# Moving a kernel's weight splitting and elementwise work from GpSimd to ScalarE and VectorE

## The chip, the cores and the metric

The kernel runs on one core of one Trainium2 chip. Its time is the device time of one execution in microseconds (us), and the median over runs is compared. Five engines work side by side on the core, each through its own instructions in order: TensorE (PE, with its weight loads shown apart as PEld), VectorE (DVE), ScalarE (ACT), GpSimd (POOL) and SyncE (SP), which here issues most DMAs.

## The reference

Two layers over 512 latent and 256 context tokens of 2048 channels. Each layer normalizes, modulates (shift, scale and gate come from a product of a condition vector with `mod_w`), mixes tokens, and adds the gated result to its input.

```python
for i in range(DEPTH):                                   # 2 layers
    shift, scale, gate = jnp.split(sc @ mod_w[i] + mod_b[i], 3, axis=-1)
    h_lat = rms_norm(x, norm_g[i]) * (1.0 + scale[:, None]) + shift[:, None]
    ...
    if i % N_MIXERS == 0:
        y_lat, y_ctx = rglru_mixer(h_lat, h_ctx, ...)    # h @ w_in, 4-tap convolution, gates, two scans, @ w_out
    else:
        y_lat, y_ctx = diff_attn_mixer(h_lat, h_ctx, ...)  # h @ w_in, q/k norm, rotary, 2 softmaxes, @ w_out
    x = x + gate[:, None] * y_lat
```

## The kernel before

Every product with a large weight is made of three matmuls: a float32 value is split into a high part in the matmul's format (a cast) and a low part (the value minus the high part), and high x high, high x low and low x high are summed in PSUM. `split` (line 43) issues the two instructions, the cast at L47 if it goes to ScalarE or L49 if to another engine, and the subtraction at L50. `weights` (line 52) fetches one weight unit of 128 x 1024 floats (512 KB) by a DMA from SP's queue into a tile `raw` (two buffers), and splits it into `wh` and `wl` (five buffers each; in the attention one unit in six has a further pair). A `raw` buffer is free for the next DMA when the subtraction has read it.

The stages in order:

- The prologue makes the RMS rows and the shift and scale of the first layer, and starts the first projections.
- The first mixer (`phase1`) works channel block by channel block, 16 of them. For a block it projects two half-blocks (`proj`: 16 channel tiles, six matmuls each, lines L327 to L331), copies the first into a padded row `up`, convolves it over time with four taps (`lru_conv`: the first tap and the bias at L426, three more on VectorE at L428, then the split into `xh` and `xl`), multiplies by the gate weights (`gps`, lines L451 to L453, three matmuls for each of eight pieces), and goes through sigmoid, tanh, exp, square and square root on ScalarE and products and scans on VectorE (lines L455 to L481). The output of a block is multiplied by its gated half (`lru_out`, lines L489 to L495). Beside that VectorE sums the modulation of the second layer (`mod_vec`, L102, one weighted sum of 512 columns after the other), spread over the blocks.
- `phase2` multiplies by `w_out` (lines L557 to L559) in four column chunks, while VectorE sums the gate of the layer for the same chunk (L102 again); a matmul with ones (L522, `gps<-ma,ones`) ends each gate. Then come the norm and the transposes of the second layer (`h_evac`).
- `phase3` goes through 16 heads. For a head the projections (lines L692 to L694, `pj`) of k and v and then of q and the gate take four weight units each; between them stands the attention of the head before: scores (L755), softmax (L757 to L765), transposes (L778), products with v (lines L790 to L792). `qk_norm` norms q and k and applies rotary positions; its four products with the sine table are at L715.
- The last head runs beside the first output columns, and `phase4` makes the others.

The order on each engine is fixed when the program is built: a scheduler places instructions by a model of the engines, so a change of engine for one kind of work moves others too. Where a line below names `hi_eng` and `lo_eng`, it is the engines of the cast and of the subtraction: in general VectorE and GpSimd, in the attention VectorE for every second subtraction too, and beside the last head ScalarE for the cast.

Of the kernel before, what the change touches and what calls it, by code (L numbers as in the profile page):

```python
# [29 lines left out]
# the last head's attention and the units of the first output columns beside it ("."), in order:  # L30
# q: channels, s: scores, t: transposes, v: times v, o: back to rows, f: norm, y: output
# [5 lines left out]
class Kern:  # L37
# [5 lines left out]
    def split(self, raw, hi, lo, hi_eng, lo_eng):  # L43
        """raw (float32) == hi + lo, both float32r"""
        nc = self.nc
        if hi_eng is nc.scalar:
            nc.scalar.copy(hi, raw)  # L47
        else:
            hi_eng.tensor_copy(hi, raw)  # L49
        return lo_eng.tensor_tensor(lo, raw, hi.bitcast(F32), op=ALU.subtract)  # L50

    def weights(self, src, shape, hi_eng=None, lo_eng=None):
        """one weight unit [128, 1024] from DRAM, split in two"""
        nc, wp = self.nc, self.wp
        raw = self.raw()
        self.wdma = nc.sync.dma_start(raw, src)
        self.wn += 1
        if self.wx is not None and self.wn % 6 == 0:
            h = self.wx.tile([128, 1024], F32R, tag="whx", name="wh")
            l = self.wx.tile([128, 1024], F32R, tag="wlx", name="wl")  # L60
        else:
            h = wp.tile([128, 1024], F32R, tag="wh", bufs=5, name="wh")
            l = wp.tile([128, 1024], F32R, tag="wl", bufs=5, name="wl")
        self.split(raw, h, l, hi_eng or nc.vector, lo_eng or nc.gpsimd)
        f = lambda t: t.rearrange("p (k c) -> p k c", k=shape[0])
        return f(h), f(l)
# [7 lines left out]
    def rsqrt(self, pool, v, n, pre, bufs=1):  # L74
        """v ** -0.5 of a small tile: a guess from the bits of v, then Newton's steps"""
# [12 lines left out]
    def mod_vec(self, ch, pool, nm, bufs=1):  # L88
        """512 columns of silu(c) @ mod_w: sums over the channel tiles, one per partition"""
# [18 lines left out]
    def mod_stream(self, pool, chunks):  # L108
        """shift and scale of layer 1: four channel tiles per chunk"""
# [33 lines left out]
    def mod_cols(self, layer, part, ch):  # L143
        """sums of the partials, channel-major: [128 channels, (latent, context)] x 2"""
        nc = self.nc
        ps = self.psum("mcol")
        for s in range(2):
            nc.tensor.matmul(ps[:, 2 * s:2 * s + 2], part[:, 128 * s:128 * s + 128], self.sel, start=True, stop=True)
        for s in range(2):
            self.mod_col(layer, 2 * ch + s, ps[:, 2 * s:2 * s + 2])  # L150

# [52 lines left out]
    def htile(self, kt, g):  # L204
        """high and low parts of 128 channels of 384 tokens"""
        return self.hp.tile([128, 2, 384], F32R, tag=f"h{kt}{g}", name=f"h{kt}{g}")

    def h_evac(self, layer, kt, g, ps, pool):
        """h = rms * A + B for one channel tile of a token group; ps: the transposed rms rows"""
# [6 lines left out]
        self.split(t, h[:, 0, :], h[:, 1, :], nc.vector, nc.gpsimd if g and kt % 2 == 0 else nc.vector)  # L216

    def norm_group(self, layer, g, kts, xt, pool):
        """transposes the rms rows of three token tiles, for the channel tiles kts, into h"""
# [22 lines left out]
    def rows(self, t, unit):  # L242
        """rms rows of one token tile, transposed"""
# [30 lines left out]
    def pairs(self, pool, unit):  # L274
        """shift and scale of layer 0 for two channel tiles at a time; behind them, h of these
        tiles and their part of the first three half-blocks"""
# [69 lines left out]
    def phase1(self, early):  # L346
# [3 lines left out]
        with tc.tile_pool(name="p1", bufs=1, reuse_waits="tile") as pool:  # L350
# [8 lines left out]
            def padded(b, uo):  # L359
                """[2 zeros, latent, 4 zeros, context, 1 zero]"""  # L360
# [35 lines left out]
    def lru_consts(self, pool):  # L396
        nc, cp = self.nc, self.c1
        # 8 softplus(-lambda), both signs
# [22 lines left out]
    def lru_conv(self, b, u, pool):  # L421
# [4 lines left out]
        nc.gpsimd.tensor_scalar(xc, u[:, 2:2 + UL], cw[:, b, 2:3], self.convb[:, b:b + 1], op0=ALU.mult, op1=ALU.add)  # L426
# [5 lines left out]
    def lru_block(self, b, x, pool):  # L432
# [3 lines left out]
        if b % 2 == 0:  # L436
            raw = self.wp.tile([128, 1024], F32, tag="raw", bufs=2, name="graw")
            nc.sync.dma_start(raw, a["gate_w"][b // 2])
            self.gates = tl("gh", 1, 1024, F32R), tl("gl", 1, 1024, F32R)
            self.split(raw, *self.gates, nc.vector, nc.gpsimd)  # L440
# [18 lines left out]
        for d in range(2):  # L459
# [4 lines left out]
            # 1 - a^2 = tanh(-log a) (1 + a^2)  # L464
# [19 lines left out]
    def lru_out(self, b, go, pool):  # L484
        """y = (sum of both directions) * silu(g)"""
# [15 lines left out]
    def y_tiles(self, kts, pool):  # L501
        """the mixer's output back as tiles of h, split"""
# [11 lines left out]
    def mod_gate(self, layer, n, pool, nm, gbufs=1):  # L514
        """512 columns of the gate, on all partitions: [128, nm, 512]"""
# [9 lines left out]
    def gate_rows(self):  # L525
        """the gate of layer 1, one row of 256 columns after the other, to DRAM"""
# [106 lines left out]
    def att_tables(self, pool):  # L633
        """gain times cosine and sine for q and k, spilled: [128, cos q, sin q, cos k, sin k]"""
# [26 lines left out]
        # lambda and the output norm's gain  # L661
# [21 lines left out]
    def qkv_mm(self, w, t, ps=None, kts=range(KT)):  # L683
        """one token tile times 256 columns"""
# [12 lines left out]
    def qk_norm(self, raw, nt, nm):  # L697
        """RMS over the 64 of each head half, gain, rotary positions; raw [128, nt, 128] in place"""
# [14 lines left out]
        for h in range(2):  # L713
            for c in range(2):
                nc.gpsimd.tensor_tensor(tv[:, :, c, :, h, :], xv[:, 0:4, c, :, 1 - h, :], sv[:, :, :, h, :], op=ALU.mult)  # L715
# [6 lines left out]
    def k_channels(self, kraw, k):  # L722
        """k [128, 2 halves, 768]: half c has its high parts on its own 64 partitions, its low parts on the other 64"""
# [10 lines left out]
    def q_channels(self, qraw, q):  # L734
        """q [128 = (part 64, the same 64), (high, low), 2 halves, 512]"""
# [32 lines left out]
    def attend_t(self, qt, st):  # L768
        """the attention of one query tile, transposed and split: [128, (high, low), 6 key tiles, 2 query tiles, 128]"""
# [13 lines left out]
    def attend_v(self, v, st):  # L783
        """the outputs of two query tiles, transposed"""
# [12 lines left out]
    def attend_o(self, pair, st):  # L797
        """back to rows"""
# [41 lines left out]
    def ytiles(self, hd):  # L840
        """the tiles of one head's output: tokens 0-383, tokens 384-511"""
# [7 lines left out]
    def yload(self, u):  # L849
        """the outputs of heads 2u and 2u + 1, split"""  # L850
# [15 lines left out]
    def early_out(self):  # L866
        """the first output columns, from all heads but the last, for two pairs of token tiles"""
# [3 lines left out]
        for pair in ((0, 1), (2, 3)):  # L871
            acc = {t: self.ppool.tile([128, 512], F32, tag="pj", bufs=2, name="acc") for t in pair}
            for u in range(8):
                if pair[0] == 0:
                    self.yload(u)
                w = self.weights(a["w_o"][0, u], (2, 512), nc.scalar, nc.vector if u % 2 else None)
# [25 lines left out]
    def head(self, hd, prev, rest, done):  # L902
        """projections of head hd, between them the attention of the head before"""
# [55 lines left out]
        w = [self.weights(a["w_kv"][hd, u], (4, 256), None, nc.vector if u % 2 and hd else None) for u in range(4)]  # L959
# [42 lines left out]
        w = [self.weights(a["w_qg"][hd, u], (4, 256), None, nc.vector if u % 2 else None) for u in range(4)]  # L1002
# [64 lines left out]
def layout(inp):  # L1067
# [6 lines left out]
    # shift and scale of layer 0: [16 chunks, 4 units, 128, 4 k-tiles, 256]  # L1074
    o["mod_w"] = c(f["mod_w"][0, :, :4096].reshape(4, 4, 128, 16, 256).transpose(3, 0, 2, 1, 4))
    # gate of layer 0; shift, scale and gate of layer 1: [16 chunks, 8 units, 128, 2 k-tiles, 512]
# [4 lines left out]
    # half-blocks u0 g0 u1 g1 ..: [32, 2, 128, 8, 128]  # L1081
# [12 lines left out]
    # [4 column chunks, 8 units, 128, 2 k-tiles, 512]  # L1094
    wo = lambda w: c(w.reshape(8, 2, 128, 4, 512).transpose(3, 0, 2, 1, 4).reshape(4, 8, 128, 1024))
    o["w_o"] = wo(f["att_w_out"][0])
    # [16 heads, 4 units, 128, 4 k-tiles, (k, v) or (q, g)]
# [26 lines left out]
```

## Time and profile before

| | |
|---|---|
| Time, median of 3 runs (lowest, highest) | 2505.36 us (2503.09, 2505.61) |
| Profiled execution: span from first to last instruction | 2499.5 us |
| TensorE busy with matmuls | 2350.4 us, 94% of the span |
| VectorE busy | 1875.8 us, 75% |
| ScalarE busy | 858.5 us, 34% |
| GpSimd busy | 694.9 us, 28% |
| Mean granted TensorE clock | 0.975 of full speed |

The profiled execution has its span alone on record, 2499.5 us; it lies 5.9 us under the median of the runs, since the span begins with the first instruction and ends with the last. Busy shares are over the whole span, and the stages have different limits, so each stage is to be read by itself.

### The profile page before, as it was taken

The numbers are of one execution on the slowest core, as the hardware profiler recorded it, in microseconds if no ns is written. First come the engines' busy times: TensorE is split into PE (matmuls) and PEld (weight loads), VectorE is DVE, ScalarE is ACT, GpSimd is POOL, SyncE is SP. The second block draws the span as 40 slices with busy tenths as digits, with TensorE's granted clock in tenths as the row PEclk, the third lists the DMA queues.
The fourth block names the chain that finished last, engine by engine and source line by source line (L and its number), as shares of the span: only waits on it lengthen the run. The fifth ranks groups of instructions, "written<-read, shape, count | busy, mean of one in ns | idle before, by whom it ended". The sixth has DMA issues, their size and how long they took to land.

```text
span 2499.5 us, 39647 instructions
## 1 busy us (share of the span) xinstructions
PE 2350.4 (94%) x15744; PEld 2197.3 (88%) x15744; DVE 1875.8 (75%) x3292; ACT 858.5 (34%) x1826; POOL 694.9 (28%) x390
## 2 busy tenths in 40 slices
PE   5989998989889899799999999999999999998899
PEld 4679998989889788679999999999999999997687
DVE  6457999999997866786787777778677766767622
ACT  4346535435337100033333333333333333235400
POOL 1243343433332233333121111212121211211352
PEclk8999999999999999999999999999999999999999
DMA  9912344434333655431232232322222211213552
GB/s 355 364 60 89 125 127 135 133 125 135 129 122 108 232 191 176 144 119 58 70 97 65 89 98 62 92 81 85 89 81 89 80 52 57 68 43 115 181 184 76
DMA packets 106473, 298.83 MB, mean 120 GB/s; under 512 B 12320, under 2 KB 33072, under 8 KB 106288
## 3 DMA queue, kind: packets, MB, share of 16 engines
q1 hardware_dynamic: 101536, 287.33, 35.2%
q10 hardware_dynamic: 4752, 8.98, 1.0%
q8 instruction: 123, 2.02, 0.3%
q14 instruction: 62, 0.51, 0.1%
HBM read 277.45 MB, written 18.82 MB: 119 GB/s over the span
## 4 chain that ended last, share of the span: by engine, by line
PE 42%; DVE 9%; DMA 3%; issue 2%; ACT 1%; POOL 1%; SPq 0%; DVEq 0%; ACTq 0%; POOLq 0%
PE pj L694 9%; PE pj L693 9%; PE pj L692 9%; PE sc L755 3%; PE acc L557 2%; DVE wh L49 2%; PE acc L558 2%; PE acc L559 2%; PE atr L778 1%; DMA raw<-w_kv 1%; DVE wl L50 1%; DMA raw<-w_o 1%; PE o L792 1%; PE o L791 1%; PE o L790 1%
## 5 line engine op out<-in xcount | busy, mean ns | idle before, releaser
L50 POOL TENSOR_TENSOR wl<-raw,wh 128x1024 fp32r<-128x1024 f32 x202 | 533.8, 2643 | 1334.8 <-DVE wh L49 975.1
L692 PE MATMUL pj<-wh,h 128*128 128x256 f32 x2560 | 730.2, 285 | 3.3 <-DVE v L50 2.7
L694 PE MATMUL pj<-wh,h 128*128 128x256 f32 x2560 | 729.2, 285 | 0.2
L693 PE MATMUL pj<-wl,h 128*128 128x256 f32 x2560 | 729.1, 285 | 0.0
L692 PEld LDWEIGHTS pj<-wh,h 128*128 128x128 f32 x2560 | 489.9, 191 | 6.2 <-DVE v L50 2.9
L693 PEld LDWEIGHTS pj<-wl,h 128*128 128x128 f32 x2560 | 490.2, 192 | 4.5 <-issue 2.6
L694 PEld LDWEIGHTS pj<-wh,h 128*128 128x128 f32 x2560 | 490.2, 191 | 3.1 <-issue 0.4
L49 DVE CAST wh<-raw 128x1024 fp32r<-128x1024 f32 x256 | 212.6, 832 | 173.4 <-PE acc L559 82.0
L102 DVE SCALAR_TENSOR_TENSOR ma<-mw,scT,ma 128x512 f32<-128x512 f32 x360 | 310.5, 906 | 18.9 <-DMA mw<-mod_v 18.9
L327 PE MATMUL proj<-h,wh 128*128 128x384 f32 x1024 | 265.5, 340 | 6.9 <-DVE h L49 6.9
L329 PE MATMUL proj<-h,wh 128*128 128x384 f32 x1024 | 271.6, 337 | 0.0
L331 PE MATMUL proj<-h,wl 128*128 128x384 f32 x1024 | 270.4, 336 | 0.0
L327 PEld LDWEIGHTS proj<-h,wh 128*128 128x128 f32 x1024 | 185.5, 190 | 15.2 <-DVE h L49 11.1
L329 PEld LDWEIGHTS proj<-h,wh 128*128 128x128 f32 x1024 | 187.2, 189 | 4.2 <-issue 2.0
L331 PEld LDWEIGHTS proj<-h,wl 128*128 128x128 f32 x1024 | 186.9, 189 | 0.8 <-issue 0.8
L761 ACT ACTIVATE p<-sc,mx 128x768 f32<-128x768 f32 x128 | 114.5, 904 | 113.1 <-DVE mx L757 108.1
L557 PE MATMUL acc<-wh,h 128*128 128x512 f32 x384 | 152.4, 398 | 0.0
L757 DVE TENSOR_REDUCE mx<-sc 128x2 f32<-128x1536 f32 x64 | 112.1, 1752 | 52.5 <-PE sc L755 52.3
L558 PE MATMUL acc<-wl,h 128*128 128x512 f32 x384 | 150.4, 392 | 0.1
L559 PE MATMUL acc<-wh,h 128*128 128x512 f32 x384 | 149.8, 391 | 0.0
L47 ACT CAST athl<-atr 128x512 fp32r<-128x512 f32 (+1 forms) x128 | 55.7, 483 | 196.7 <-PE atr L778 196.5
L755 PE MATMUL sc<-k,q 128*128 128x512 f32 (+1 forms) x512 | 108.2, 339 | 2.5 <-ACT p L761 2.5
(241 smaller groups left out, 3942.8 us busy)
## 6 DMA issues: line engine op xcount, KB each, us to landing
mw<-mod_v SPq DMA_DIRECT2D x96, 512.0 KB, 3.8
mw<-mod_w SPq DMA_DIRECT2D x64, 512.0 KB, 9.8
raw<-w_in SPq DMA_DIRECT2D x64, 512.0 KB, 3.6
raw<-w_kv SPq DMA_DIRECT2D x64, 512.0 KB, 3.7
raw<-w_qg SPq DMA_DIRECT2D x64, 512.0 KB, 3.9
raw<-w_out SPq DMA_DIRECT2D x40, 512.0 KB, 4.3
raw<-w_o SPq DMA_DIRECT2D x40, 512.0 KB, 3.5
raw<-mod_v SPq DMA_DIRECT2D x64, 256.0 KB, 3.6
```

What stands on the lines that cost most here:

```text
L49: hi_eng.tensor_copy(hi, raw)
L50: return lo_eng.tensor_tensor(lo, raw, hi.bitcast(F32), op=ALU.subtract)
L102: nc.vector.scalar_tensor_tensor(acc[m], w[:, k, :], sc, acc[m], op0=ALU.mult, op1=ALU.add)
L327: nc.tensor.matmul(ps[g][:, :384], wh, h[g][:, 0, :], start=first, stop=False)
L329: nc.tensor.matmul(ps[g][:, :384], wh, h[g][:, 1, :], start=False, stop=False)
L331: nc.tensor.matmul(ps[g][:, :384], wl, h[g][:, 0, :], start=False, stop=last)
L557: nc.tensor.matmul(acc[t], yh, wh, start=(kt == first), stop=False)
L558: nc.tensor.matmul(acc[t], yh, wl, start=False, stop=False)
L559: nc.tensor.matmul(acc[t], yl, wh, start=False, stop=(kt == last))
L692: nc.tensor.matmul(ps, h[:, 0, c], wh, start=(kt == 0), stop=False)
L693: nc.tensor.matmul(ps, h[:, 0, c], wl, start=False, stop=False)
L694: nc.tensor.matmul(ps, h[:, 1, c], wh, start=False, stop=(kt == KT - 1))
```

## The change

Every weight unit is cast on ScalarE and its low part subtracted on VectorE, whatever the stage. The gate weights of the first mixer (`graw`) go the same way. The first convolution tap, until now a GpSimd instruction, becomes a ScalarE activation with scale and bias. The four sine products of `qk_norm` go to VectorE, and so does the low part of h in `h_evac` where GpSimd had it. GpSimd keeps memory sets at the start and the one-time tables of `att_tables`.

```diff
-    def weights(self, src, shape, hi_eng=None, lo_eng=None):
+    def weights(self, src, shape):
...
-        self.split(raw, h, l, hi_eng or nc.vector, lo_eng or nc.gpsimd)
+        self.split(raw, h, l, nc.scalar, nc.vector)
...
-        self.split(t, h[:, 0, :], h[:, 1, :], nc.vector, nc.gpsimd if g and kt % 2 == 0 else nc.vector)
+        self.split(t, h[:, 0, :], h[:, 1, :], nc.vector, nc.vector)
...
-        nc.gpsimd.tensor_scalar(xc, u[:, 2:2 + UL], cw[:, b, 2:3], self.convb[:, b:b + 1], op0=ALU.mult, op1=ALU.add)
+        nc.scalar.activation(xc, u[:, 2:2 + UL], AF.Identity, scale=cw[:, b, 2:3], bias=self.convb[:, b:b + 1])
...
-            self.split(raw, *self.gates, nc.vector, nc.gpsimd)
+            self.split(raw, *self.gates, nc.scalar, nc.vector)
...
-                nc.gpsimd.tensor_tensor(tv[:, :, c, :, h, :], xv[:, 0:4, c, :, 1 - h, :], sv[:, :, :, h, :], op=ALU.mult)
+                nc.vector.tensor_tensor(tv[:, :, c, :, h, :], xv[:, 0:4, c, :, 1 - h, :], sv[:, :, :, h, :], op=ALU.mult)
...
-                w = self.weights(a["w_o"][0, u], (2, 512), nc.scalar, nc.vector if u % 2 else None)
+                w = self.weights(a["w_o"][0, u], (2, 512))
...
-        w = [self.weights(a["w_kv"][hd, u], (4, 256), None, nc.vector if u % 2 and hd else None) for u in range(4)]
+        w = [self.weights(a["w_kv"][hd, u], (4, 256)) for u in range(4)]
...
-        w = [self.weights(a["w_qg"][hd, u], (4, 256), None, nc.vector if u % 2 else None) for u in range(4)]
+        w = [self.weights(a["w_qg"][hd, u], (4, 256)) for u in range(4)]
```

VectorE's order in one block of the first mixer, from the second convolution tap (`xc<-up`) to the output product (`sg`), before; `a` and `r` are tiles of the scans:

```order
L428 SCALAR_TENSOR_TENSOR xc<-up_1668,conv_wT,xc 128x772
L479 SCALAR_TENSOR_TENSOR a_3560<-a_3560,r_3506 128x512
L428 SCALAR_TENSOR_TENSOR xc<-up_1668,conv_wT,xc 128x772
L49 CAST wh<-raw 128x1024
L481 TENSOR_TENSOR a_3549<-a_3549,a_3560 128x772
L49 CAST xh<-xc 128x772
L50 TENSOR_TENSOR xl<-xc,xh 128x772
L49 CAST wh<-raw 128x1024
L492 SCALAR_TENSOR_TENSOR sg<-sg,proj 128x384 x2
L494 TENSOR_TENSOR sg<-a_3549,sg 128x512
```

The same place on VectorE in the change:

```order
L428 SCALAR_TENSOR_TENSOR xc<-up_1668,conv_wT,xc 128x772
L50 TENSOR_TENSOR wl<-raw,wh 128x1024
L479 SCALAR_TENSOR_TENSOR a_3560<-a_3560,r_3506 128x512
L428 SCALAR_TENSOR_TENSOR xc<-up_1668,conv_wT,xc 128x772
L481 TENSOR_TENSOR a_3549<-a_3549,a_3560 128x772
L49 CAST xh<-xc 128x772
L50 TENSOR_TENSOR xl<-xc,xh 128x772
L50 TENSOR_TENSOR wl<-raw,wh 128x1024
L492 SCALAR_TENSOR_TENSOR sg<-sg,proj 128x384 x2
L494 TENSOR_TENSOR sg<-a_3549,sg 128x512
```

Each cast of `raw` has made room for a subtraction that reads `raw` and `wh`; the recurrence around it stands as it did.

ScalarE's order at the same block, from the square root (L468) to the next block's gates (L455), before:

```order
L468 ACT_TABLE_LOAD
L468 ACTIVATE r_3505<-r_3505 128x772
L466 ACTIVATE sq<-a_3560 128x772
L468 ACTIVATE r_3506<-r_3506 128x772
L361 COPY up_1668<-proj 128x384
L362 COPY up_1668<-proj 128x128
L363 COPY up_1668<-proj 128x256
L489 ACT_TABLE_LOAD
L489 ACTIVATE sg<-proj 128x384 x2
L455 ACT_TABLE_LOAD
```

And in the change:

```order
L468 ACT_TABLE_LOAD
L468 ACTIVATE r_3505<-r_3505 128x772
L466 ACTIVATE sq<-a_3560 128x772
L47 CAST wh<-raw 128x1024
L361 COPY up_1668<-proj 128x384
L362 COPY up_1668<-proj 128x128
L363 COPY up_1668<-proj 128x256
L468 ACTIVATE r_3506<-r_3506 128x772
L426 ACTIVATE xc<-up_1668,conv_bT,conv_wT 128x772
L47 CAST wh<-raw 128x1024 x2
L489 ACT_TABLE_LOAD
L489 ACTIVATE sg<-proj 128x384 x2
```

Three weight casts and the first tap have come in, and the second square root has moved behind the copies into `up`.

## Rows read from the trace of the kernel before

**Rows 1.** The page: busy us, share of the span, instructions of each engine.

```profile
PE 2350.4 (94%) x15744; PEld 2197.3 (88%) x15744; DVE 1875.8 (75%) x3292; ACT 858.5 (34%) x1826; POOL 694.9 (28%) x390
```

**Rows 2.** Busy time by stretch: start:end, length, engines, clock, DMA share, GB/s.

```profile
165.80:372.80 207.00, 193.94 (x1074) 192.05 (x1072) 182.39 (x195) 118.49 (x157) 82.86 (x39) 0.96 0.34 111
372.80:741.40 368.60, 329.37 (x1826) 324.35 (x1824) 357.28 (x427) 162.27 (x216) 132.08 (x45) 0.94 0.41 131
...
786.00:1045.80 259.80, 252.91 (x1112) 207.91 (x1110) 188.95 (x238) 44.02 (x88) 77.56 (x31) 0.99 0.57 185
1045.80:1190.00 144.20, 122.20 (x819) 110.78 (x818) 111.41 (x193) 42.37 (x93) 52.07 (x32) 0.93 0.32 99
1190.00:2205.00 1015.00, 1002.60 (x8167) 985.58 (x8166) 754.63 (x1593) 334.58 (x943) 201.26 (x164) 1.00 0.25 77
2205.00:2360.00 155.00, 139.51 (x905) 123.44 (x904) 110.18 (x227) 69.56 (x166) 38.37 (x25) 0.97 0.34 107
```

**Rows 3.** Waits of PE, whole run: total us, times, longest us.

```profile
PE gps L451 <- DVE xh L49: 32.1, 9, 7.8
PE gps L522 <- DVE ma L102: 20.0, 2, 13.2
PE gps L452 <- DVE xl L50: 17.0, 12, 2.5
```

**Rows 4.** Two short stretches of the first mixer, columns as in rows 2.

```profile
300.00:331.00 31.00, 31.00 (x181) 31.00 (x180) 30.82 (x35) 14.46 (x20) 13.01 (x4) 1.00 0.39 120
373.00:380.00 7.00, 0.83 (x3) 0.43 (x2) 6.96 (x7) 0.00 (x0) 3.10 (x1) 0.81 0.50 150
```

**Rows 5.** Timeline of DVE in one block: start, us, what.

```profile
398.30 2.88 DVE L102 SCALAR_TENSOR_TENSOR ma<-mw,scT,ma 128x512 f32<-128x512 f32 x1
...
401.98 1.40 DVE L102 SCALAR_TENSOR_TENSOR ma<-mw,scT,ma 128x512 f32<-128x512 f32 x2
...
417.91 0.99 DVE L428 SCALAR_TENSOR_TENSOR xc<-up,conv_wT,xc 128x772 f32<-128x772 f32 x1
```

**Rows 6.** Timeline of POOL over the same time.

```profile
397.07 3.56 POOL L50 TENSOR_TENSOR wl<-raw,wh 128x1024 fp32r<-128x1024 f32 x1 [14.06 <-PE proj L331]
```

**Rows 7.** DVE by line, 372.9 to 741.4 (eight blocks): count, busy us, mean ns, idle before.

```profile
L102 DVE SCALAR_TENSOR_TENSOR ma<-mw,scT,ma 128x512 f32<-128x512 f32 x184 | 153.8, 874 | 8.8 <-DMA mw<-mod_v 8.8
L428 DVE SCALAR_TENSOR_TENSOR xc<-up,conv_wT,xc 128x772 f32<-128x772 f32 x25 | 37.5, 1500 | 0.0
L49 DVE CAST wh<-raw 128x1024 fp32r<-128x1024 f32 x33 | 22.3, 677 | 0.0
L467 DVE SCALAR_TENSOR_TENSOR r<-sq,r 128x772 f32<-128x772 f32 x16 | 21.8, 1362 | 0.0
L494 DVE TENSOR_TENSOR sg<-a,sg 128x512 f32<-128x512 f32 x8 | 17.6, 2196 | 0.3
L475 DVE TENSOR_TENSOR_SCAN a<-a,r 128x512 f32<-128x512 f32 x8 | 16.2, 2025 | 0.0
L50 DVE TENSOR_TENSOR xl<-xc,xh 128x772 fp32r<-128x772 f32 x8 | 15.8, 1979 | 0.3
...
L479 DVE TENSOR_TENSOR_SCAN a<-a,r 128x512 f32<-128x512 f32 x9 | 11.4, 1271 | 0.0
...
L481 DVE TENSOR_TENSOR a<-a,a 128x772 f32<-128x772 f32 x8 | 7.6, 948 | 0.0
```

**Rows 8.** Groups by line, whole run: POOL's sine products for k, ACT's cast.

```profile
L715 POOL TENSOR_TENSOR rt<-kraw,tab 128x128 f32<-128x128 f32 x64 | 41.9, 684 | 173.6 <-ACT kraw L968 93.6 <-DVE l L762 79.9
...
L47 ACT CAST wh<-raw 128x1024 fp32r<-128x1024 f32 x16 | 16.8, 1050 | 16.9 <-DMA raw<-w_o 15.4 <-POOL rt L715 1.4
```

**Rows 9.** The chain that ended last: a subtraction on DVE with POOL idle.

```profile
1983.15 1.23 DVE wl L50
```

**Rows 10.** Timeline of DVE around the last gate of the first layer.

```profile
1011.20 0.69 DVE L49 CAST wh<-raw 128x1024 fp32r<-128x1024 f32 x1 [7.47 <-PE acc L559]
1059.04 0.68 DVE L49 CAST wh<-raw 128x1024 fp32r<-128x1024 f32 x1
```

## The prediction

> **What bounds the kernel now.** I read the page's busy times first: TensorE is busy 94% of the span, VectorE 75%, GpSimd 28% [rows 1]. So at most about 149 us (2499.5 less 2350.4) are idle on TensorE, and a change that moves elementwise work can only win there, and in what the clock loses after a pause. Where these idle times lie is read from the busy times by stretch [rows 2]. In the heads TensorE is busy 1002.6 of 1015 us at full clock, so there is next to nothing to win and something to lose. In the eight blocks of the first mixer from 372.8 to 741.4 it is different: TensorE is busy 329.4 of 368.6 us at a granted clock of 0.94, and VectorE 357.3, which is 97%. The chain of who waits for whom says the same: TensorE waits for the split of the convolution's result, 32.1 us for the high part and 17.0 for the low part [rows 3], almost all of it in this mixer. A pause costs more than its length: in the 7 us around one such wait TensorE works 0.83 us and the clock falls to 0.81 of full [rows 4], that is, part of the stretch is at the 1.2 GHz level. So VectorE bounds the first mixer, and TensorE the rest, apart from two gates of `phase2` (20.0 us of waiting in two waits, the longer 13.2 [rows 3]).
>
> The next view is VectorE's own timeline. Two weighted sums of 512 columns take 1.40 us together, 0.70 each, but one of the same form takes 2.88 us [rows 5]. It lies inside a GpSimd subtraction that runs from 397.07 to 400.63 [rows 6], and it ends about when that does. The groups by line show how much of this there is [rows 7]: a scan of 512 takes 1271 ns at one line and 2025 at another; two-input products over 772 take 948 ns at L481 and 1362 at L467; the subtraction of `xl`, of the same length, takes 1979. While GpSimd computes, some of VectorE's instructions with two tensors from SBUF stand still.
>
> **The change part by part.** All per block of the first mixer, an eighth of the stretch with eight of them, 46.1 us long, with VectorE busy 44.7.
>
> 1. GpSimd's instructions go, and with them the standstill. Over the eight blocks [rows 5, 7]: L102 has 184 at 153.8/184 = 0.836 us against 0.70, 25.0 us; L428 25 at 1.50 against 0.99, 12.8; L467 16 at 1.362 against 0.948, 6.6; L494 8 at 2.196 against 0.948 x 512/772 = 0.63, 12.5; L475 8 at 2.025 against 1.271, 6.0; `xl` 8 at 1.979 against 0.948, 8.2. Sum 71.1, or 8.9 a block. If only the long ones at L494, `xl` and L428 came back it would be 4.2 a block; that is the lower bound.
>
> 2. The casts leave VectorE: 22.3/8 = 2.8 us a block [rows 7]. Subtractions come: 33 in eight blocks, 4.1 a block, at 1.23 us when GpSimd is idle [rows 9], 5.1 us. The gate weights, one unit in two blocks, do the same: half of 1.23 less 0.68, 0.3. VectorE then has 44.7 - 8.9 - 2.8 + 5.1 + 0.3 = 38.4 us a block.
>
> 3. TensorE: 31.0 us of matmuls without a pause at full clock hold 181 of them [rows 4], 171 ns each; a block has 1826/8 = 228 [rows 2], so 39.1 us. TensorE becomes the bound, with VectorE just under it.
>
> 4. ScalarE takes the casts at 1050 ns [rows 8], 4.6 a block with the gates, 4.8 us, and the first tap, for which 0.79 us (772/1024 of the cast) to 1.6 us (twice that) are the bounds; I take 1.0, since it is one pass over one input like the cast. With 162.3/8 = 20.3 us now [rows 2] it comes to 26.1 of about 40. The order shows that the casts stand in ScalarE's queue between the square root and the copies of the projections: what is behind them, the copies into `up` and the next block's gates, waits a microsecond more for each. The buffers hide that, as five weight units are ahead of TensorE, which needs one every 10 us; without that cover it would be 4.6 x 1.05 = 4.8 us a block.
>
> With VectorE at 38.4 and TensorE at 39.1, both in order, I take a block as 40.0 us: 6.1 less, 49 us for eight. The bounds are 39.1 (56 us) and, if the loss in 1 is only halved, 38.4 + 4.7 = 43.1 on VectorE alone (24 us).
>
> A rule of the Trainium skill speaks against part of this: the page "ScalarE: Activation LUTs", section "Rules for kernel authors", gives plain adds and multiplies to VectorE rather than ScalarE, as faster per element. The trace agrees as to the length, 1050 ns against 677. By that rule the casts would stay on VectorE: 38.4 + 2.8 + 0.3 = 41.5 us a block, the mixer bound there again, and some 20 us of the 49 gone. The rows speak for ScalarE, because it has half of a block free.
>
> 5. Before these blocks, 165.8 to 372.8, 1074 matmuls need 184 of 207 us [rows 2, 4]. VectorE has 182.4 us busy and little of the stream of weighted sums yet. I take half of the 23 us, 12; the bounds are 5 and 23.
>
> 6. In `phase2` the last gate is late because VectorE works from 1011.2 to 1059.0 without a real pause [rows 10], 47.8 us. A fifth of that (8.9 of 44.7) is 9.6 us of standstill; eight subtractions for eight casts cost 8 x (1.23 - 0.68) = 4.4 more. The net is 5.2, which I round up to 6, since many of the instructions there are the exposed L102. For the other, shorter gate 4 of 6.8 us (20.0 less 13.2), and 2 us of clock: 12; bounds 5 and 24.
>
> 7. From 1045.8 to 1190 TensorE idles 22.0 us, 13.2 of them the gate above. Of the other 8.8 I take 3, for the low part of h on VectorE (bounds 0 and 8.8).
>
> 8. Heads: 12.4 us idle [rows 2]. VectorE is at 74% of the stretch. Per head, eight casts leave (5.4 us), four subtractions come (4.9), and eight sine products. Their price is between 128/1024 of the subtraction, 0.15 us, and GpSimd's 0.68 [rows 8]; I take 0.3, 2.4 us a head. What hides them is VectorE's free quarter and that the norm's products stand before transposes which TensorE reaches after more projections. Uncovered, 16 heads would cost 38 us. ScalarE goes from 334.6 to about 334.6 + 14 x 8 x 1.05 = 452 of 1015 us. I take 0, from 12 gained to 10 lost.
>
> 9. Last head and first output columns: 15.5 us idle [rows 2]; GpSimd's subtractions lie in the way from DMA to matmul there, 6 us. Everything else (prologue, the end of the mixer, `phase4`): 5. No transfer is added, and SP's queue keeps its DMAs; each waits for a `raw` buffer that is now freed by VectorE.
>
> The sum is 49 + 12 + 12 + 3 + 0 + 6 + 5 = 87 us off the span of 2499.5: 2412.5. The runs' median of 2505.4 lies 5.9 us above that span, so the forecast for the runs is 2418 us.
>
> **The rivals.**
>
> A. The mixer keeps a wait: VectorE and ScalarE hand work to each other in both directions in a block, both in order, and with a cast more in that loop the block comes to about 43 us in place of 40. For it speaks that VectorE's 38.4 leave TensorE's 39.1 no room, and that ScalarE's casts must now come before VectorE's subtractions. Against it: five buffers of weights. It gives 24 us less in the eight blocks and 8 less elsewhere: 2450 us.
>
> B. The other side: the heads lose. TensorE has 99% there. Each head changes its weight units twice, and with five or six buffers the last two units of a set can only be split once the set before lets a buffer go. If the cast then stands in ScalarE's queue behind an exponential or a copy that waits for TensorE, TensorE waits at each change. 32 changes pay off the 87 us at 2.7 us each; at 3.5 us it would be 112 lost, 2530 us. Against it: cast plus subtraction take 1.05 + 1.23 us, hardly more than 0.68 + 1.23 now on the units that VectorE splits alone, and ScalarE has half its time free.
>
> C. The standstill is no lock but chance: VectorE's times stay. Then a block has 44.7 - 2.8 + 5.4 = 47.3 us of VectorE, 1.2 more than its present length, about 10 us in all for eight blocks, 2515 us. The 2.88 us inside GpSimd's 3.56 [rows 5, 6] speak against that.
>
> D. All waits of mixer and gates go: 56 + 23 + 24 + 9 + 0 + 10 + 8 = 130 us, 2375 us.
>
> **How the numbers follow.** Forecast (2400 to 2437): 0.58. A: 0.21. D: 0.09. B: 0.08, of which 0.06 slower. C: 0.04, half of it slower. A difference below 0.2%, about 5 us, can't be told from none here. Faster: 0.58 + 0.21 + 0.09 = 0.88; slower 0.06 + 0.02 = 0.08; within 0.2%: 0.04. The range leaves out half of D below, so 2385; above it reaches past A, to 2470, and leaves out B and C. The likeliest case by itself is 2400 to 2437.
>
> **What would show it.** Step 1: weighted sums at L102 of about 740 ns mean in the mixer, and none near 2.9 us. Steps 2 and 3: VectorE below 39 us a block, the eight blocks at about 40 us each, PE's waits for `xh` and `xl` (49 us) below 15, a clock near 0.99 in that stretch. Step 6: the wait of 13.2 us down to about 6. Step 8: the heads' stretch of 73 us each unchanged. The prediction is wrong if L102 keeps its long pieces, if TensorE's waits in the mixer now name ScalarE's casts or the subtraction, or if the heads grow by more than 1 us each.

## The result and the profile after

The changed kernel takes 2405.95 us (median of 4 runs, 2404.44 to 2409.26), against 2505.49 us (2503.09 to 2505.68) for the kernel before, measured with it: a ratio of 0.9606, 95% interval 0.9592 to 0.962. It is 4% faster, and 12 us below the 2418 us of the forecast. The profiled execution went from a span of 2499.5 to 2402.7 us, 96.8 less. The page's first row shows which engines have less to do, to be held against [rows 1]:

```profile
PE 2321.4 (97%) x15744; PEld 2179.0 (91%) x15744; DVE 1667.9 (69%) x3382; ACT 1147.0 (48%) x2115; POOL 8.4 (0%) x20
```

TensorE has the same 15744 matmuls and 29 us less busy time, VectorE has 90 instructions more and 208 us less busy time, ScalarE 289 us more. GpSimd has 8.4 us left. Busy time by stretch answers rows 2; the stretches are cut at the same events in both traces: the first gate matmul of the first mixer (L451), of its seventh block, the first matmul of `w_out` after its last block, the last gate of `phase2` (L522), and the first transpose of q (L739) in the first and the last head. Columns: start:end, length, TensorE, its weight loads, VectorE, ScalarE, GpSimd, granted clock, share of the DMA engines, GB/s.

```profile
164.70:360.60 195.90, 189.03 (x1062) 187.84 (x1061) 157.35 (x203) 147.12 (x186) 6.16 (x12) 0.97 0.36 117
360.60:672.30 311.70, 311.70 (x1826) 311.70 (x1825) 299.22 (x426) 215.39 (x268) 0.00 (x0) 1.00 0.48 154
672.30:726.50 54.20, 54.20 (x318) 54.10 (x317) 32.89 (x51) 40.34 (x56) 0.00 (x0) 1.00 0.31 99
726.50:977.00 250.50, 237.10 (x1023) 191.94 (x1021) 170.08 (x241) 68.17 (x105) 0.00 (x0) 0.98 0.59 193
977.00:1106.60 129.60, 122.28 (x835) 111.97 (x836) 85.23 (x198) 59.14 (x111) 0.00 (x0) 0.95 0.28 87
1106.60:2195.30 1088.70, 1085.29 (x8811) 1066.13 (x8811) 740.84 (x1808) 482.83 (x1154) 0.00 (x0) 1.00 0.25 78
2195.30:2402.70 207.40, 185.41 (x826) 150.44 (x824) 93.30 (x135) 60.06 (x95) 0.00 (x0) 0.98 0.44 144
```

The trace of before, cut at the same events, for the six and the eight blocks, the heads and the last stretch:

```profile
166.70:378.70 212.00, 193.91 (x1072) 192.05 (x1072) 187.39 (x198) 118.49 (x157) 85.95 (x40) 0.96 0.34 111
378.70:745.20 366.50, 329.38 (x1824) 324.35 (x1824) 355.18 (x427) 162.27 (x216) 131.59 (x44) 0.95 0.41 130
...
1193.90:2294.60 1100.70, 1084.43 (x8795) 1063.84 (x8795) 817.59 (x1743) 368.59 (x1035) 218.43 (x179) 1.00 0.25 77
2294.60:2499.50 204.90, 189.70 (x836) 153.66 (x836) 88.95 (x131) 36.28 (x72) 72.70 (x30) 0.96 0.46 148
```

The balance, in us:

| stretch | before | after | gain | forecast |
|---|---|---|---|---|
| to the first gate | 166.7 | 164.7 | 2.0 | part of 5 |
| six mixer blocks | 212.0 | 195.9 | 16.1 | 12 |
| eight mixer blocks | 366.5 | 311.7 | 54.8 | 49 |
| end of the mixer | 56.4 | 54.2 | 2.2 | part of 5 |
| gates of `phase2` | 257.4 | 250.5 | 6.9 | 12 |
| norm, start of the heads | 134.9 | 129.6 | 5.3 | 3 |
| heads, 15 periods | 1100.7 | 1088.7 | 12.0 | 0 |
| last head and output | 204.9 | 207.4 | -2.5 | 6, part of 5 |

More than half of the gain is in the eight blocks: TensorE is busy there for 311.70 of 311.70 us at clock 1.00. Of the 54.8 us, 37.1 are TensorE's idle time, and 17.7 are the same matmuls done faster, since the clock no longer falls (0.95 before, 1.00 now). Its waits over the whole run (total, times, longest) are now these:

```profile
PE gps L522 <- DVE ma L102: 13.3, 2, 8.0
PE tps L266 <- DVE v L254: 12.1, 1, 12.1
PE proj L327 <- DVE h L49: 6.6, 6, 2.3
...
PE acc L557 <- ACT wh L47: 4.1, 4, 1.5
PE gps L451 <- ACT i L457: 3.5, 1, 3.5
```

The two waits for the halves of the convolution, `xh` and `xl`, 49.1 us before [rows 3], are gone from the list. VectorE's groups in the eight blocks (count, busy us, mean ns, idle before) answer rows 7:

```profile
L102 DVE SCALAR_TENSOR_TENSOR ma<-mw,scT,ma 128x512 f32<-128x512 f32 x184 | 129.7, 745 | 2.1 <-DMA mw<-mod_v 2.0
L50 DVE TENSOR_TENSOR wl<-raw,wh 128x1024 fp32r<-128x1024 f32 x32 | 38.8, 1214 | 0.0
L428 DVE SCALAR_TENSOR_TENSOR xc<-up,conv_wT,xc 128x772 f32<-128x772 f32 x24 | 24.2, 1009 | 0.0
L467 DVE SCALAR_TENSOR_TENSOR r<-sq,r 128x772 f32<-128x772 f32 x16 | 15.4, 960 | 5.1 <-ACT sq L466 5.0
...
L475 DVE TENSOR_TENSOR_SCAN a<-a,r 128x512 f32<-128x512 f32 x8 | 10.2, 1279 | 0.0
...
L50 DVE TENSOR_TENSOR xl<-xc,xh 128x772 fp32r<-128x772 f32 x8 | 7.7, 958 | 0.1
```

The same instructions on the same data are shorter than in rows 7: L428 1500 to 1009 ns, the scan 2025 to 1279, `xl` 1979 to 958.

### The profile page after: what moved, and what is told of

The parts are those of the page before. It is cut to its first block, busy times and chain, and to the rows that moved or that the text cites. A ratio compares the mean times of both kernels' runs of the same rounds, so it can differ in the third digit from the quotient of the medians.

```text
span 2402.7 us, 39516 instructions
## 1 busy us (share of the span) xinstructions
PE 2321.4 (97%) x15744; PEld 2179.0 (91%) x15744; DVE 1667.9 (69%) x3382; ACT 1147.0 (48%) x2115; POOL 8.4 (0%) x20
## 4 chain that ended last, share of the span: by engine, by line
PE 84%; DMA 5%; DVE 5%; ACT 4%; issue 1%; SPq 0%; ACTq 0%; DVEq 0%
PE pj L692 12%; PE pj L693 12%; PE pj L694 12%; PE proj L327 7%; PE proj L329 7%; PE proj L331 7%; PE acc L557 4%; PE acc L558 4%; PE acc L559 4%; PE sc L755 4%; PE atr L778 2%; DVE wl L50 1%; DMA raw<-w_o 1%; ACT wh L47 1%; PE mps L295 1%
## 5 line engine op out<-in xcount | busy, mean ns | idle before, releaser
L47 ACT CAST wh<-raw 128x1024 fp32r<-128x1024 f32 x272 | 285.0, 1051 | 473.2 <-PE acc L559 163.6
L50 DVE TENSOR_TENSOR wl<-raw,wh 128x1024 fp32r<-128x1024 f32 x272 | 331.4, 1221 | 202.3 <-ACT wh L47 201.9
L102 DVE SCALAR_TENSOR_TENSOR ma<-mw,scT,ma 128x512 f32<-128x512 f32 x360 | 252.1, 745 | 12.8 <-DMA mw<-mod_v 12.6
```

The lines of the kernel that those rows point to most:

```text
L102: nc.vector.scalar_tensor_tensor(acc[m], w[:, k, :], sc, acc[m], op0=ALU.mult, op1=ALU.add)
```

## The experiments

Each kernel is an edit of the changed kernel ("after" below). All do the whole computation, and two add work to it. The blocks are the eight of the table, cut at the same events.

### Casts back on VectorE

```diff
-        self.split(raw, h, l, nc.scalar, nc.vector)
+        self.split(raw, h, l, nc.vector, nc.vector)
...
-            self.split(raw, *self.gates, nc.scalar, nc.vector)
+            self.split(raw, *self.gates, nc.vector, nc.vector)
```

> The changed kernel with the casts of weights and gate weights back on VectorE; GpSimd stays idle. Theory (VectorE's load and GpSimd's standstill both bound the first mixer): VectorE goes from the changed kernel's 37.4 us of work a block to 37.4 + 4.6 x 0.61 = 40.2, above TensorE's 39.0, so a block takes 41 to 42 us and the kernel 2430 to 2450 us. Rival 1 (only the standstill counted, VectorE's load has room): 2406 us, within 5. Rival 2 (the gain was ScalarE taking the casts, and nothing else): most of the 99 us go, 2480 or more.

Measured: 2422.08 us (2419.77 to 2426.74), ratio 0.9663 [0.9647, 0.9679], 16 us above after: less than the theory expected, and more than rival 1. The view by stretch, of the eight blocks and of a piece behind them, and TensorE's longest wait between 670 and 740:

```profile
360.00:678.90 318.90, 315.91 (x1837) 312.99 (x1835) 305.40 (x443) 169.09 (x224) 0.00 (x0) 1.00 0.45 144
692.10:714.90 22.80, 0.25 (x2) 0.00 (x0) 22.43 (x30) 11.82 (x16) 0.00 (x0) 0.60 0.35 113
...
PE mcol L115 <- DVE ma L102: 22.8, 1, 22.8
```

A block takes 39.9 us, hardly more than after's 39.0. But VectorE did only 164 of the 184 weighted sums of L102 in the eight blocks, and the rest piled up behind them: TensorE stands for 22.8 us until they are done, and the mixer's end takes 78.0 us in place of 54.2. A block's length alone would have hidden this. Together the two stretches lose 31.0 us; the stages behind the mixer are 8.1 us shorter in this execution.

### Low parts back on GpSimd

```diff
-        self.split(raw, h, l, nc.scalar, nc.vector)
+        self.split(raw, h, l, nc.scalar, nc.gpsimd)
...
-            self.split(raw, *self.gates, nc.scalar, nc.vector)
+            self.split(raw, *self.gates, nc.scalar, nc.gpsimd)
```

> The changed kernel with all low parts of weights and gate weights on GpSimd, casts on ScalarE. Theory: VectorE loses 4.6 subtractions a block (5.3 us) and gets the standstill back (up to 8.9 us a block), so 37.4 - 5.3 + 8.9 = 41.0 us of work, a block of 41 to 43 us, L102 back at 850 ns or more, and 2435 to 2465 us. Rival 2 (it is the casts that had to leave VectorE): VectorE has 32 us a block, the mixer stays at TensorE's 39 us a block and the kernel at 2406 to 2415 us.

Measured: 2469.05 us (2467.2 to 2469.38), ratio 0.9852 [0.9837, 0.9867], a little over the theory's range; the blocks take 343.3 us, 42.9 each, the heads 1106.6. The eight blocks by stretch, and the groups of L102 and of GpSimd there:

```profile
376.20:719.50 343.30, 321.21 (x1824) 316.85 (x1824) 335.12 (x392) 215.81 (x268) 103.71 (x36) 0.98 0.41 139
...
L102 DVE SCALAR_TENSOR_TENSOR ma<-mw,scT,ma 128x512 f32<-128x512 f32 x184 | 176.7, 1007 | 5.9 <-DMA mw<-mod_v 5.9
...
L50 POOL TENSOR_TENSOR wl<-raw,wh 128x1024 fp32r<-128x1024 f32 x32 | 92.6, 2895 | 183.1 <-ACT wh L47 183.1
```

VectorE has 34 instructions fewer than after and is busy for 36 us more. Freeing it of work made it slower: 63.1 of the 99.5 us that the change gave are lost again, though the casts stay on ScalarE. The casts alone are not what helps.

### A bystander on GpSimd with two inputs, and one with one input

Both add GpSimd work that nobody reads, 64 instructions of 512 columns in the eight blocks, and nothing else; in these blocks the instructions of TensorE, VectorE and ScalarE and their order are those of after, row for row. Ahead of the blocks one memory set stands elsewhere in the first kernel, and a few instructions in the second. `self.by` is true only from the start of the first mixer to its last block; `scp` is a tile that nothing else uses there.

```diff
+        if self.by:
+            v = self.scp.rearrange("p k c -> p (k c)")
+            for i in range(2):
+                nc.gpsimd.tensor_tensor(v, h.bitcast(F32)[:, 512 * i:512 * i + 512], v, op=ALU.add)
```

The other has, in place of the last line, one input and a constant:

```diff
+                nc.gpsimd.tensor_scalar(v, h.bitcast(F32)[:, 512 * i:512 * i + 512], 0.5, None, op0=ALU.mult)
```

> The changed kernel and, in the first mixer alone, two more GpSimd instructions per weight unit that nobody waits for: each adds 512 columns of the high part to a tile that is no longer used. VectorE's order is the same, row for row. Theory (GpSimd's two-input work holds up VectorE): some 2 x 1.2 us x 4.1 units = 9.9 us a block on GpSimd, of which most stand on VectorE: 37.4 + 6 to 9 us a block, blocks of 44 to 47 us, 2450 to 2490 us. Rival 3 (the gain came from the new order or from the shorter way to the low part): nothing changes, 2406 us within 5.

> The same with GpSimd instructions of one input (512 columns of the high part times 0.5). Theory: in the trace of before a one-input tap of 3.61 us let several of VectorE's instructions through, so it holds them up less: a block of 39 to 41 us, 2406 to 2430 us. If any GpSimd work holds VectorE up to its whole length, it is as the two-input one. Rival 3: 2406 us.

With two inputs: 2493.79 us (2493.15 to 2495.73), ratio 0.9954 [0.9939, 0.9968], 87.8 of the 99.5 us gone, 4 us more than the theory's range. A block takes 46.2 us, before's was 45.8. The eight blocks, VectorE's first two groups, GpSimd's only one, and TensorE's largest wait (in these two kernels L102 of after stands at L107, L451 at L458):

```profile
390.00:759.20 369.20, 329.86 (x1824) 325.06 (x1824) 364.95 (x430) 215.72 (x268) 109.40 (x64) 0.94 0.40 130
...
L107 DVE SCALAR_TENSOR_TENSOR ma<-mw,scT,ma 128x512 f32<-128x512 f32 x184 | 164.5, 933 | 2.2 <-DMA mw<-mod_v 1.9
L51 DVE TENSOR_TENSOR wl<-raw,wh 128x1024 fp32r<-128x1024 f32 x32 | 44.9, 1402 | 0.5 <-ACT wh L48 0.5
...
L69 POOL TENSOR_TENSOR scp<-wh,scp 128x512 f32<-128x512 f32 x64 | 109.4, 1709 | 261.9 <-ACT wh L48 259.3
...
PE gps L458 <- DVE xh L50: 49.6, 11, 6.8
```

The waits of before are back, and the clock at 0.94, with no instruction of VectorE added or moved in these blocks. The bystander also reads `wh` and could hold that buffer back, but that does not explain it: one wait of 1.9 us, of ScalarE's cast, is all that the waits show for it, and the kernel with one input has the same. Outside the mixer, where there is no bystander, the stages are after's (`phase2` 250.7, heads 1088.5). The timelines of GpSimd and VectorE at one place (start, us):

```profile
406.34 3.48 POOL L69 TENSOR_TENSOR scp<-wh,scp 128x512 f32<-128x512 f32 x2 [22.43 <-ACT wh L48]
...
406.89 3.49 DVE L107 SCALAR_TENSOR_TENSOR ma<-mw,scT,ma 128x512 f32<-128x512 f32 x2
```

Two sums that take 1.41 us in the clear take 3.49 here, and end 0.56 us after GpSimd (410.38 against 409.82).

With one input: 2426.26 us (2422.11 to 2429.7), ratio 0.9682 [0.9667, 0.9698], a block 40.8 us. GpSimd is busy for longer, and VectorE loses a third as much:

```profile
364.30:690.60 326.30, 316.50 (x1827) 312.55 (x1825) 321.57 (x429) 215.16 (x268) 123.71 (x64) 0.99 0.46 147
...
380.54 3.43 POOL L69 TENSOR_SCALAR scp<-wh 128x512 f32<-128x512 f32 x2 [19.18 <-ACT wh L48]
...
380.84 1.77 DVE L107 SCALAR_TENSOR_TENSOR ma<-mw,scT,ma 128x512 f32<-128x512 f32 x2
382.53 1.37 DVE L476 SCALAR_TENSOR_TENSOR i<-i,xc 128x772 f32<-128x772 f32 x1
```

While two of these run on GpSimd, VectorE finishes two sums in 1.77 us (1.41 in the clear) and a product in 1.37 (0.95): it is held for some 0.4 us for each of GpSimd's instructions, and the rest of their time is free. VectorE's busy time rises from 299.2 us to 365.0 with two inputs, 1.03 us for each of the 64 instructions of 1.71 us, and to 321.6 with one, 0.35 us for each of 1.93. (The profile's spans of GpSimd are rough; the rise of VectorE's busy time does not rest on them.)

### The heads' splits and sine products as before

```diff
-        w = [self.weights(a["w_kv"][hd, u], (4, 256)) for u in range(4)]
+        w = [self.weights(a["w_kv"][hd, u], (4, 256), nc.vector, nc.vector if u % 2 and hd else nc.gpsimd) for u in range(4)]
...
-        w = [self.weights(a["w_qg"][hd, u], (4, 256)) for u in range(4)]
+        w = [self.weights(a["w_qg"][hd, u], (4, 256), nc.vector, nc.vector if u % 2 else nc.gpsimd) for u in range(4)]
```

with the sine products (L715) on GpSimd; and a second kernel with only those moved back:

```diff
-                nc.vector.tensor_tensor(tv[:, :, c, :, h, :], xv[:, 0:4, c, :, 1 - h, :], sv[:, :, :, h, :], op=ALU.mult)
+                nc.gpsimd.tensor_tensor(tv[:, :, c, :, h, :], xv[:, 0:4, c, :, 1 - h, :], sv[:, :, :, h, :], op=ALU.mult)
```

> The changed kernel with the heads' weights and sine products on the engines of before: casts on VectorE, low parts on GpSimd and VectorE in turn, sine products on GpSimd. Theory (the same standstill, hidden by VectorE's free time but for the chains that TensorE waits for): the heads from 1106 to 2195 us, 1088.7 us in the changed kernel, go back to about the 1100.7 of before, TensorE's idle time there from 3 to about 15 us, and the kernel to 2414 to 2422 us. Rival (the heads were shortened by the order alone, or by where the earlier stages ended): 2406 us within 4.

> The changed kernel with the sine products alone on GpSimd. Theory: they are 4.7 us of GpSimd work a head, just ahead of the products on VectorE that they hold up, so part of the 12 us in the heads comes back: heads 1091 to 1099 us, the kernel 2408 to 2417 us. Rival (the low parts alone did the harm in the heads): heads 1088 to 1090 us, 2406 us within 3.

As before: 2432.09 us (2430.36 to 2434.33), ratio 0.9709 [0.9696, 0.9723], a greater loss than theory or rival expected; why it is more than the 12.0 us that the heads had gained stays open. The heads take 1107.2 us, 18.5 more than after, TensorE idles there for 20.0 us (16.3 before, 3.4 after), and the eight blocks stay at 39.0 each. The heads by stretch, and TensorE's largest waits inside them, which are short ones as before:

```profile
1113.50:2220.70 1107.20, 1087.16 (x8798) 1065.98 (x8798) 816.64 (x1746) 370.91 (x1039) 212.42 (x177) 1.00 0.24 77
...
PE otr L826 <- DVE ot L819: 4.5, 4, 1.3
PE qtr L739 <- DVE qraw L719: 3.8, 2, 2.4
```

The sine products alone: 2409.4 us (2408.36 to 2409.84), ratio 0.9618 [0.9605, 0.9631], heads 1089.1, as the rival had it. So in the heads the split made the loss; where the products stand costs next to nothing. Of the split it is the low parts on GpSimd: with VectorE's casts alone the last of the kernels below loses nothing.

### The first tap back on GpSimd

```diff
-        nc.scalar.activation(xc, u[:, 2:2 + UL], AF.Identity, scale=cw[:, b, 2:3], bias=self.convb[:, b:b + 1])
+        nc.gpsimd.tensor_scalar(xc, u[:, 2:2 + UL], cw[:, b, 2:3], self.convb[:, b:b + 1], op0=ALU.mult, op1=ALU.add)
```

> The changed kernel with the first convolution tap alone on GpSimd, 16 instructions of one input. Theory: one-input work holds VectorE up little (the bystander of one input, 9.9 us a block, cost 1.8 us a block), a tap of 2.6 us costs about 0.3, and the convolution starts 1.6 us later inside a slack of some 20 us: blocks of 39.0 to 39.4 us, 2406 to 2413 us. Rival (the way from projection to gates sets the block): 1.6 us more a block, 2425 to 2432 us.

Measured: 2409.39 us (2408.06 to 2412.16), ratio 0.9618 [0.9605, 0.9631], a block still 39.0 us. VectorE is busy for 2.8 us more in the eight blocks, 0.34 for each tap, close to the 0.35 of the bystander with one input, and its slack covers that. (The bystander's GpSimd time was 15.5 us a block, not the 9.9 of the expectation.)

### The last head's casts on VectorE

```diff
-                w = self.weights(a["w_o"][0, u], (2, 512))
+                w = self.weights(a["w_o"][0, u], (2, 512), nc.vector)
```

> The changed kernel with the casts of the first output columns, beside the last head, on VectorE in place of ScalarE. In the changed kernel TensorE idles 22 us after the last head has begun (15 before), and most of these pauses name ScalarE's cast, VectorE's subtraction or the softmax, which ScalarE also makes. Theory: ScalarE is crowded there by the casts of both the outputs and the weights, so 5 to 10 us come back, 2396 to 2402 us. Rival (the transfer and the two steps one behind the other set the pace, whichever engine casts): 2406 us within 3.

Measured: 2411.52 us (2410.78 to 2412.6), ratio 0.9627 [0.9614, 0.964]. From the first transpose of q in the last head to the last instruction it is 210.5 us, against 207.4 in after. It did not get shorter, so my theory that casts crowd ScalarE there falls.

### Casts on VectorE everywhere but in the mixer, and in the heads alone

The first kernel has `self.cast` on ScalarE and sets it to VectorE from `phase2` on; the second sets it to VectorE in the loop over the heads only:

```diff
-        self.split(raw, h, l, nc.scalar, nc.vector)
+        self.split(raw, h, l, self.cast, nc.vector)
...
+            self.cast = nc.vector
```

```diff
+            self.cast = self.nc.vector if hd < HEADS else self.nc.scalar
```

> The changed kernel with ScalarE casting the weights in the prologue and the first mixer alone, and VectorE casting them in all later stages; GpSimd idle. From the run with all casts on VectorE: its norm stretch, heads and end were 3.5, 3.0 and 2.1 us shorter than the changed kernel's (126.1, 1085.7, 202.0 against 129.6, 1088.7, 204.1), and only its mixer lost (29 us). Theory (where TensorE bounds and VectorE has room, the shorter cast is a little better, 0.69 us against 1.05): 2397 to 2403 us, a kernel better than both. Rival (these few us are the chance of one profiled execution and of the order): 2404 to 2410 us.

> The same for the 16 heads alone, ScalarE casting in all other stages. Theory: only the 3.0 us of the heads, 2402 to 2405 us. Rival: 2404 to 2410 us; if ScalarE's exponentials were held up by the casts it would be more, below 2400 us.

Measured: 2404.21 us (2401.07 to 2405.23), ratio 0.9596 [0.9583, 0.9609], and 2403.16 us (2397.47 to 2405.8), ratio 0.9586 [0.9573, 0.9599]. Both intervals overlap that of after: outside the mixer the engine of the cast makes no difference that can be measured, and neither is a better version. The first misses its theory; the second lies where theory and rival can't be told apart. The heads do look 3 us shorter with VectorE's casts, which was the theory's ground:

```profile
1113.30:2198.50 1085.20, 1082.51 (x8782) 1063.72 (x8781) 813.75 (x1927) 367.22 (x1034) 0.00 (x0) 1.00 0.25 78
```

But this stretch of the first kernel holds 29 matmuls fewer than after's 8811, and the stretch before it 27 more (862 for 835): the order moved work across the cut, and TensorE's idle time is 2.7 us for 3.4.

## Why the prediction was right, step by step

**The standstill (step 1).** Shown. The bystander with two inputs brings the old block length back with VectorE's own program unchanged, so rival C (chance) is out, and a new order is not needed to explain the gain. That the length comes out nearly equal is in part my choice of the bystander's load (109.4 us of GpSimd work for before's 131.6). L102 fell to 745 ns, as forecast. How one-sided the bargain was shows with the low parts back on GpSimd: the 36 subtractions are 43.7 us less of VectorE's work (36 x 1.214), and its busy time is 35.9 us more, so that it stands still for 79.6 of the 103.7 us that GpSimd works.

**VectorE, TensorE and ScalarE per block (steps 2 to 4).** VectorE is at 299.22/8 = 37.4 us for 38.4 forecast, TensorE at 39.0 for 39.1, ScalarE at 215.39/8 = 26.9 for 26.1. TensorE is the bound, without one pause, so the block is 39.0 and not 40.0: the microsecond that I allowed for leftover waits was not needed, and the term is 54.8 us in place of 49. Rival A is out, and rival D right about these blocks (56), not about the gates. The casts on VectorE cost 16 us where I had worked out 20, but by another way, through the backlog of sums at the mixer's end and hardly through longer blocks. The cast is 1045 ns on ScalarE against 693 on VectorE; the longer instruction won where VectorE had no room, and where it had, the last two kernels show nothing either way. The Trainium skill, page "ScalarE: Activation LUTs", section "Rules for kernel authors", gives `add` and `mul` to VectorE rather than ScalarE, as faster per element; its row names no cast. The runs agree as to the length of one instruction, and not as to the engine on which this mixer is faster.

**The earlier stretch (step 5).** 16.1 us for 12, inside the bounds of 5 and 23. Idle time fell by 11.2 us (18.1 to 6.9) and busy time by 4.9. Of the 4.9 some 1.8 are no gain: ten matmuls of 0.18 us moved ahead of the cut (1062 for 1072), into the stretch to the first gate. The rest is the clock (0.96 to 0.97).

**The gates of `phase2` (step 6).** 6.9 us for 12. The longer wait fell from 13.2 to 8.0, close to the 6 us taken off it in the forecast. The other fell from 6.8 to 5.3 only, where I had taken off 4, and the 2 us for the clock gave 0.5 (busy 237.57 to 237.10).

**The norm (step 7)** gave 5.3 for 3, inside its bounds.

**The heads (step 8)** are the step that failed: 12.0 us for 0, at the edge of its bounds, and by my estimate nearer 14 at equal work, as 16 matmuls more stand in the stretch now (8811 for 8795, at 0.12 us each). I counted the instructions that come and go on VectorE, +1.9 us a head, and put the standstill there at nothing. VectorE's busy time fell by 76.8 us over 15 heads, 5.1 a head. In the traces of before and after, in the heads:

```profile
L49 DVE CAST wh<-raw 128x1024 fp32r<-128x1024 f32 x115 | 106.9, 930 | 46.0 <-DMA raw<-w_qg 22.6 <-PE pj L694 14.5 <-DMA raw<-w_kv 8.1
...
L765 DVE SCALAR_TENSOR_TENSOR p<-p,l 128x768 f32<-128x768 f32 x60 | 78.4, 1306 | 0.3
```

```profile
L765 DVE SCALAR_TENSOR_TENSOR p<-p,l 128x768 f32<-128x768 f32 x60 | 60.9, 1015 | 0.7
```

The casts that left had cost 930 ns each, not the 677 of the mixer's rows; put back without GpSimd, in the last of the experiments (where L50 is the cast), they take 688:

```profile
L50 DVE CAST wh<-raw 128x1024 fp32r<-128x1024 f32 x114 | 78.5, 688 | 42.2 <-PE pj L695 17.6 <-DMA raw<-w_qg 14.1 <-DMA raw<-w_kv 6.9
```

And the product and sum at L765 fell from 1306 to 1015. With that the short waits went, and TensorE's idle time from 16.3 to 3.4 us. Rival B (lost heads) is out.

**The last head (step 9)** has the wrong sign: 2.5 us longer, not 6 shorter. TensorE's busy time fell by 4.3 us, some 2 of them ten matmuls that moved ahead of the cut (826 for 836), and its idle time rose from 15.2 to 22.0, of which one wait of 5.9 for the probabilities (L765). The 6 us of the forecast rested on GpSimd's subtractions in the way to the matmul. TensorE had waited 2.4 us for them and 0.6 for the casts; now it waits 1.3 and 2.1 for the two, so the term was set at more than the wait. That the casts crowd ScalarE was refuted by the run with the last head's casts on VectorE. With the casts of the heads alone on VectorE this stretch is 204.3 us, with the same wait (6.1), so the length hangs in part on the heads ahead of it. What makes it stays open.

The sum was right to 10 us in part by luck: four terms were too small (blocks 5.8, earlier stretch 4.1, norm 2.3, heads 12.0: 24 us) and others too large (gates 5.1, and step 9, where the prologue's 2.0, the mixer's end with 2.2 and the last head's -2.5 make 1.7 of 11). The other 2 to 3 of the 12 us come from setting the runs 5.9 us above the span. It is not the counting from the first instruction to the last that makes 5.9: in every run for which both are on record the time lies 1.7 to 2.2 us above the span, so the profiled execution of before was some 4 us quicker than the median run. For after the median lies 3.3 above the profiled span.

## What to carry to other kernels

Before giving work to an idle GpSimd, look in VectorE's timeline for instructions of one form that differ in length, and see whether the long ones lie inside GpSimd's: the price of GpSimd's work is then paid by VectorE, also by instructions that have nothing to do with it, and here it counted in the heads too, where VectorE is not the bound. Where VectorE was full, a longer instruction on an engine with free time was the better place (the casts, 16 us). And compare a stage together with the one behind it, and count its matmuls, since a scheduler can push work over the border, as the 22.8 us at the mixer's end and the 29 matmuls of the heads show.

## What the runs showed of the hardware

Which of VectorE's instructions stand still goes with where their inputs lie and with who starts first. At one place in the first mixer of before (start, us; the third line is GpSimd's timeline):

```profile
380.33 1.01 DVE L492 SCALAR_TENSOR_TENSOR sg<-sg,proj 128x384 f32<-128x384 f32 x2
381.37 2.19 DVE L494 TENSOR_TENSOR sg<-a,sg 128x512 f32<-128x512 f32 x1
...
380.64 2.37 POOL L50 TENSOR_TENSOR wl<-raw,wh 128x1024 fp32r<-128x1024 f32 x1 [4.00 <-PE gps L452]
```

GpSimd's subtraction begins before the second of the two products at L492, which read one tile in SBUF and one in PSUM; they take 0.54 us each, as in after (547 ns). The product at L494 reads two tiles in SBUF: it takes 2.19 us, where after has 0.69, and ends 0.55 us after GpSimd. It is the same in all eight blocks (rows 7 have 2196 ns for L494).

A VectorE cast, which has one input, was held up too: 930 ns in the heads of before, 928 with the heads' splits as before, 688 there with GpSimd idle. One of the held casts in the heads of before, and GpSimd's subtraction beside it:

```profile
1249.96 2.81 DVE L49 CAST wh<-raw 128x1024 fp32r<-128x1024 f32 x1 [0.27 <-PE pj L694]
...
1249.82 2.39 POOL L50 TENSOR_TENSOR wl<-raw,wh 128x1024 fp32r<-128x1024 f32 x1 [20.95 <-DVE wh L49]
```

It begins 0.14 us after GpSimd and ends 0.56 us after it. In the eight blocks of before the casts kept their 677 ns: there the casts that met a GpSimd subtraction had begun 0.2 us before it, and the others that met GpSimd ran beside the first tap, which has one input.

How long GpSimd holds VectorE went with GpSimd's own kind of instruction: 1.03 us for each 1.71 with two inputs, 0.35 us for each 1.93 with one. The two bystanders differ in the operation as well as in the number of inputs, so it is not shown that the second input alone makes the difference. The Trainium skill, page "SBUF — State Buffer", section "SBUF: two separate sides", says that of a VectorE instruction with two inputs in SBUF and a GpSimd instruction that reads SBUF the one that starts first shuts the other out for the whole of its instruction. The runs come near that for two inputs on GpSimd (1.03 us lost for each 1.71, and an end 0.56 us behind GpSimd's), and do not agree for one: there VectorE goes on after some 0.4 us while GpSimd runs for 1.9.

GpSimd's own instructions vary too: with all low parts there, a subtraction of 1024 columns takes 2895 ns in the eight blocks, where VectorE is busy 98% of the time, and 2539 over the whole run.
